# ScalarE for the first norm's second token block, and row halves that alternate in the indexer scores, in a two-layer fp32 decoder

## The chip, the cores and the metric

The kernel runs on one core of a Trainium2 chip. The metric is the device time of one execution, in microseconds (us). The time of the kernel before is 927.51 us, the median of 3 runs (927.25 to 927.71).

## What is computed

The reference is a post-norm decoder of two layers on 256 tokens of 1,024 channels, in fp32, with a LayerNorm ahead of the first layer. The parts that the change touches:

```python
h = _layer_norm(x, ln_in_g, ln_in_b)
# per layer: h <- LN(alpha*h + Mixer(h)); h <- LN(alpha*h + ConvGatedMLP(h))
# A: logits += cumsum(log sigmoid forget gate), causal softmax, times v
# B, the indexer that picks 64 keys per query:
r = relu(einsum('bqhd,bkd->bqhk', q_idx, k_idx) * DI ** -0.5)
score = einsum('bqhk,bqh->bqk', r, w_idx)
# C, differential attention:
p = softmax(s, axis=-1)
a = p[:, :, 0] - lam * p[:, :, 1]
o_c = _rms_norm(einsum('bhqk,bkhd->bqhd', a, v), diff_norm_g) * (1.0 - lam_init)
```

## The kernel before

**Weights.** About 80 MB of fp32 weights per layer stream through SBUF once. SyncE loads chunks of 512 KB into seven raw buffers. `Stream.split` (line 146) cuts each 128x512 piece into a high part, which ScalarE writes (hl <- raw), and a low part, which VectorE writes (raw minus high, hl <- raw, hl). Sixteen such pairs fit. TensorE then makes three fp32r matmuls per product (`mm3`): high x high, low x high, high x low. A pair is used by six matmuls of 512 columns, or by twelve of 256. The activations are split in the same way into hTh and hTl.

**Order.** The order of every engine's instructions is fixed when the program is built. The main line emits the weight matmuls, and after every few of them `Tasks.tick` (line 286) lets each live task, a Python generator, emit a piece of its work (attention, norms, rotary steps) and then calls `Stream.refill` (line 177), which may emit one split. When a task may go on is decided by the planner `Clocks` (line 197), which adds up modelled costs per engine. `ready(engine, tiles)` (line 387) holds a task until its inputs are done by these clocks, and also while VectorE's clock is more than 2.5 us ahead of TensorE's, and, for VectorE's tasks in the attention stage, while fewer than three pairs are split ahead. `refill` splits when fewer than `W.low` pairs are ahead, or when `W.hold` is off and VectorE's clock is not too far on. `W.low` is -1 during the first norm and LOW = 3 afterwards.

**Start.** `first_norm` (line 590) runs once per block of 128 tokens (tb = 0, 1): statistics, rs from GpSimd, two normalisations of 128x512, eight transposes on TensorE, two multiplications and additions with gb in PSUM on VectorE, then hTh (ScalarE) and hTl (VectorE). `spins` (line 585) are bf16 matmuls on a constant that nobody reads; tb = 0 has nine. The bank `warm` holds their output. Between the two calls the main line (lines 1316 to 1325) splits four pieces, two with the low part on VectorE and two on GpSimd. The rotary tables, on GpSimd and ScalarE, come behind.

**Attention.** `task_g1` (line 722) makes augL and augR, on 16 partitions, with which one matmul adds the forget-gate sums to A's logits (`task_A`, line 992: a mask matmul, the aug matmul, then the scores, for three banks per layer). `task_index` (line 859) makes the indexer's scores, 64 rows deep: heads with even numbers lie in the lower row half of the array, odd ones in the upper. A bank takes heads of one half; `par` runs two banks side by side. Relu (ScalarE) and a chain of multiply-adds into s (VectorE) follow, and then eight rounds of max and match-replace. `task_C` (line 1006) makes both softmaxes of differential attention, with the heads of the two halves in turn. `soften` (line 900) takes exponentials with their sums; the first softmax (a) is normalised there by eight operations, the second (p) is folded in by eight multiply-adds. `Square` with a sum and `crr` on GpSimd make the RMS norm of the product with v.

Every operation is issued from one helper line, L267.

Of the kernel before, what the change touches and what calls it, by code (L numbers as in the profile page):

```python
# [10 lines left out]
F32 = mybir.dt.float32  # L11
# [7 lines left out]
P = 128  # L19
# [92 lines left out]
class Stream:  # L112
# [32 lines left out]

    def split(self, lo=None):
        i = self.next_split
        if i >= len(self.items):
            return
        c, q, w = self.items[i]  # L150
        t = self.hl_pool.tile([P, 2, 512], R32, name=f"hl{i}", tag="hl")
        r = self.raw[c][:, q:q + w]
        clk = self.clocks.clk
        clk["ACT"] = max(clk["ACT"], self.free_at.get(i - HL_BUFS, 0))
        self.sc.activation(t[:, 0, :w], r, AF.Copy)
        (lo or self.ve).tensor_tensor(t[:, 1, :w], r, t[:, 0, :w].bitcast(F32), ALU.subtract)
        self.hl[i] = t
        self.next_split += 1
        if i + 1 == len(self.items) or self.items[i + 1][0] != c:
            del self.raw[c]  # L160
            self.split_at[c] = clk["DVE"]
            self.dma()

    def take(self):
# [31 lines left out]
class Clocks:  # L196
# [3 lines left out]
    def __init__(self):  # L200
        self.clk = dict(PE=0.0, DVE=0.0, ACT=0.0, POOL=0.0)
        self.done, self.by, self.read = {}, {}, {}
        self.table = "exp"

# [25 lines left out]
    def note(self, eng, op, args, kw):  # L230
# [8 lines left out]
        if op == "dma_start":  # L239
            self.done[out.name] = max(self.clk[eng], self.clk["PE"]) + 4000  # L240
            return
        start = max([self.clk[eng]] + [self.done.get(n, 0) for n in map(part, aps[1:]) if self.by.get(n) != eng])
        self.clk[eng] = start + self.cost(eng, op, out, aps)
        if "accum_out" in kw:
            self.clk[eng] += 155
# [70 lines left out]
def tile_hybrid(ctx: ExitStack, tc: tile.TileContext, a: dict, out: bass.AP):  # L316
# [273 lines left out]
    def first_norm(tb, st, hT, flag):  # L590

        mu, rs = ln_stats(st)
        if tb:
            yield
        for q in range(2):
            ve.tensor_scalar(h[tb][q], h[tb][q], mu, rs, ALU.subtract, ALU.mult)
        yield
        bks = []
        for q in range(2):
            yield from ready("PE", h[tb][q])  # L600
            bk = yield from att()
            bks.append(bk)
            transpose4(bk, h[tb][q])
            v = bk.rearrange("p (k t) -> p k t", k=4)
            for i, f in enumerate((ALU.mult, ALU.add)):
                ve.tensor_tensor(v, v, gb[:, i, 4 * q:4 * q + 4].unsqueeze(2).broadcast_to([P, 4, P]), f)
        if not tb:
            spins(9)
            att_free(warm)
        for q, bk in enumerate(bks):  # L610
            split_out(hT[0][:, 4 * q:4 * q + 4, tb * P:(tb + 1) * P],
                      hT[1][:, 4 * q:4 * q + 4, tb * P:(tb + 1) * P],
                      bk.rearrange("p (k t) -> p k t", k=4))
            att_free(bk)
            if not tb and not q:
                W.split(gp)
        flag.add(tb)
        W.hold = len(flag) < 2

    residual = set()  # L620
# [88 lines left out]
    def layer(l, hT, hflag):  # L709
# [12 lines left out]
        def task_g1(g1):  # L722
# [71 lines left out]
            t_ = t1([16, 256], "ct")  # L794
            augL = t1([16, 256], "augL", R32)
            augR = t4([16, 4, 256], R32, "augR")
            col = lambda i: cst[0:16, C_COL + i:C_COL + i + 1]
# [8 lines left out]
            for q in range(4):  # L806
                ve.tensor_scalar(augR[:, q, :], ch, cst[0:16, C_BM + q:C_BM + q + 1], None, ALU.mult)
            F["aug"] = (augL, augR)

# [49 lines left out]
        def task_index():  # L859
# [3 lines left out]
            s1 = t2([P, 256], n="s1")  # L863
            sx = [s0, s1]

            jobs = [(0, [0, 2, 4, 6]), (0, [1, 3, 5, 7]), (1, [0, 2]), (1, [1, 3]), (1, [4, 6]), (1, [5, 7])]

            def job(qb, hs):
                kw = P * (qb + 1)
                bk = yield from att()  # L870
                for n, i in enumerate(hs):
                    o = 64 * (i % 2)
                    mm(bk[:, n * kw:(n + 1) * kw], qiT[o:o + 64, i // 2, qb * P:(qb + 1) * P],
                       kiT[o:o + 64, 0:kw], n == 0)
                yield from ready("ACT", bk)
                rl = t2([P, len(hs), kw])
                sc.activation(rl, bk.rearrange("p (n k) -> p n k", n=len(hs)), AF.Relu)
                att_free(bk)
                for n, i in enumerate(hs):
                    prev = (m38[:, 256 - kw:256] if i == 0 else sx[qb])  # L880
                    ve.scalar_tensor_tensor(sx[qb], rl[:, n, :], biw[:, qb, i:i + 1], prev, ALU.mult, ALU.add)

            for i in range(0, 6, 2):
                yield from par(job(*jobs[i]), job(*jobs[i + 1]))
            mx = small([P, 2, 8], "mx")
# [13 lines left out]

        def soften(bk, ms, pt, rinv, norm=True):  # L900

# [3 lines left out]
            ve.tensor_reduce(mx[:, :len(ms)], v, AX.X, ALU.max, negate=True)  # L905
            sm = small([P, 4], "ssm")
            for n, m in enumerate(ms):
# [98 lines left out]
        def task_C():  # L1006
# [3 lines left out]
            a1, p1 = t4([P, 4, 256], n="a1"), t4([P, 4, 256], n="p1")  # L1010
            rina = small([P, 2, 4], "rina")
            rinv = small([P, 2, 4], "rinv")

            def scores(qb, ms):
# [5 lines left out]
                for n, m in enumerate(ms):  # L1020
                    for c in range(2):
                        mm(bks[c][:, n * kw:(n + 1) * kw],
                           qcT[64 * c:64 * c + 64, m, qb * P:(qb + 1) * P],
                           kcT[64 * c:64 * c + 64, m, 0:kw], False)
                yield from par(soften(bks[0], ms, (a0, a1)[qb], rina[:, qb, :]),
                               soften(bks[1], ms, (p0, p1)[qb], rinv[:, qb, :], norm=False))
            yield from par(scores(0, [0, 1, 2, 3]), scores(1, [0, 1]), scores(1, [2, 3]))
            ve.tensor_scalar(rinv, rinv, nlam[:, l:l + 1], None, ALU.mult)
            for qb, (pp, aa) in enumerate(((p0, a0), (p1, a1))):
                for m in range(4):  # L1030
                    ve.scalar_tensor_tensor(aa[:, m, :], pp[:, m, :], rinv[:, qb, m:m + 1], aa[:, m, :],
                                            ALU.mult, ALU.add)
            yield from ready("PE", a0, a1)
            q0 = t4([P, 4, 256], n="q0")
# [7 lines left out]
            def job(qb):  # L1042
# [356 lines left out]
```

## Time and profile before

| | before |
|---|---|
| median of 3 runs | 927.51 us (927.25 to 927.71) |
| profiled execution | 927.42 us |
| its span | 925.6 us |
| mean granted TensorE clock | 0.996 |
| TensorE matmul busy | 903.9 us |
| VectorE busy | 658.6 us |
| ScalarE busy | 510.4 us |
| GpSimd busy | 46.4 us |

A row of the timeline names the start, the duration of the group, the engine, the operation with its output and inputs, the shape and the count, and in brackets how long the engine sat idle before it and which engine released it. PE is TensorE's matmuls, PEld its weight loads, DVE is VectorE, ACT is ScalarE, POOL is GpSimd. An fp32 matmul stands as two records. Matmuls are pipelined, so the distance from start to start says what one costs; the duration is longer.

### The profile page before, as it was taken

How to read it: one execution, taken by the hardware profiler on the slowest of the kernel's cores; microseconds unless marked ns; L12 is line 12 of the kernel's file. 1: busy time of each engine (PE TensorE's matmuls, PEld its weight loads, DVE VectorE, ACT ScalarE, POOL GpSimd, SP SyncE). 2: the span in 40 equal slices, each digit the busy share in tenths (PEclk: the TensorE clock that was granted, in tenths of full speed). 3: DMA queues.
4: the chain of work that ended last, by engine and by line, in shares of the span. 5: the costliest groups of instructions: out<-in, count | busy, mean ns of one | idle time of the engine just before them, and what ended most of it. 6: DMA issues, size and time to landing. Idle time of an engine off the chain costs nothing. (4 is left out here: it accounts for less than half of the span.)

```text
span 925.6 us, 14457 instructions
## 1 busy us (share of the span) xinstructions
PE 903.9 (98%) x5329; PEld 787.8 (85%) x5329; DVE 658.6 (71%) x1283; ACT 510.4 (55%) x1006; POOL 46.4 (5%) x63
## 2 busy tenths in 40 slices
PE   7999999999999999999999999999999999999996
PEld 4877887888888999999988788888888799999995
DVE  7788677766678766766787956667667886766755
ACT  4754765655537655655455455665555375655540
POOL 6100000011000000000000000000110100000000
PEclk9999999999999999999999999999999999999999
DMA  8823356556636665565444323548675385566501
GB/s 289 303 91 114 95 171 231 193 199 221 204 122 225 215 200 187 180 200 182 131 157 152 113 91 114 188 138 286 187 245 172 119 277 186 177 192 186 180 18 46
DMA packets 46681, 161.47 MB, mean 174 GB/s; under 512 B 5841, under 2 KB 6865, under 8 KB 46609
## 3 DMA queue, kind: packets, MB, share of 16 engines
q1 hardware_dynamic: 44208, 155.20, 51.1%
q0 software_dynamic: 1408, 4.98, 1.7%
q8 instruction: 42, 0.69, 0.3%
q10 hardware_dynamic: 992, 0.35, 0.1%
q14 instruction: 31, 0.25, 0.1%
HBM read 159.47 MB, written 1.05 MB: 173 GB/s over the span
## 5 line engine op out<-in xcount | busy, mean ns | idle before, releaser
L267 DVE TENSOR_TENSOR hl<-raw,hl 128x512 fp32r<-128x512 f32 (+1 forms) x578 | 387.3, 696 | 186.6 <-ACT hl L267 184.7
L267 ACT ACTIVATE hl<-raw 128x512 fp32r<-128x512 f32 (+1 forms) x584 | 347.4, 625 | 192.9 <-PE att L267 94.1
L267 PE MATMUL acc<-hl,hTh 128*128 128x512 f32 (+1 forms) x896 | 276.8, 390 | 2.5 <-ACT hTh L267 2.1
L267 PE MATMUL att<-hTh,hl 128*128 128x256 f32 x1280 | 231.5, 283 | 0.0
L267 PEld LDWEIGHTS att<-hTh,hl 128*128 128x128 f32 x1280 | 200.8, 192 | 1.4
L267 PEld LDWEIGHTS acc<-hl,hTh 128*128 128x128 f32 x896 | 166.9, 188 | 37.7 <-ACT hTh L267 3.7
L267 PE MATMUL att<-hTl,hl 128*128 128x256 f32 x640 | 181.1, 283 | 0.0
L267 PE MATMUL acc<-hl,hTl 128*128 128x512 f32 (+1 forms) x448 | 165.5, 387 | 0.9 <-DVE hTl L267 0.9
L267 PE MATMUL acc<-hl,act 128*128 128x512 f32 x528 | 123.4, 390 | 0.0
L267 PEld LDWEIGHTS att<-hTl,hl 128*128 128x128 f32 x640 | 122.8, 192 | 0.0
L267 PEld LDWEIGHTS acc<-hl,act 128*128 128x128 f32 x528 | 97.9, 188 | 19.5
L267 PEld LDWEIGHTS acc<-hl,hTl 128*128 128x128 f32 x448 | 84.5, 189 | 17.7 <-DVE hTl L267 2.4
L267 PE MATMUL acc<-hl,oT 128*128 128x512 f32 x288 | 68.3, 391 | 0.0
L267 PEld LDWEIGHTS acc<-hl,oT 128*128 128x128 f32 x288 | 53.7, 188 | 10.9
L267 DVE SCALAR_TENSOR_TENSOR cv<-att,convp,cv 128x255 f32<-128x255 f32 x88 | 40.4, 480 | 16.1 <-ACT cv L267 14.5
L267 PE MATMUL acc<-hTh,hl 128*128 128x256 f32 x256 | 48.7, 289 | 3.0 <-DVE hl L267 2.6
L267 PE MATMUL acc<-hl,mT 128*128 128x512 f32 x192 | 45.4, 392 | 0.0
L267 PEld LDWEIGHTS acc<-hTh,hl 128*128 128x128 f32 x256 | 39.9, 191 | 5.5 <-DVE hl L267 3.2
L267 PEld LDWEIGHTS acc<-hl,mT 128*128 128x128 f32 x192 | 35.6, 188 | 7.1
L267 ACT ACTIVATE hTh<-att 128x512 fp32r<-128x512 f32 x16 | 9.6, 597 | 49.1 <-PE att L267 43.1
L267 PE MATMUL acc<-hTl,hl 128*128 128x256 f32 x128 | 36.2, 283 | 0.0
L267 ACT ACTIVATE t<-att 128x512 f32<-128x512 f32 (+1 forms) x32 | 18.2, 599 | 28.3 <-PE att L267 23.1
(162 smaller groups left out, 686.6 us busy)
## 6 DMA issues: line engine op xcount, KB each, us to landing
raw<-in_w_dram SPq DMA_DIRECT2D x284, 512.0 KB, 4.3
raw<-in_w_dram SPq DMA_DIRECT2D x8, 332.0 KB, 3.8
lng<-in_ln_g_dram POOLq DMA_DIRECT2D x4, 512.0 KB, 4.2
lnb<-in_ln_b_dram POOLq DMA_DIRECT2D x4, 512.0 KB, 5.5
h<-in_x_dram SPq DMA_DIRECT2D x4, 256.0 KB, 4.7
lng<-in_ln_in_g_dram SPq DMA_DIRECT2D x1, 512.0 KB, 8.1
lnb<-in_ln_in_b_dram SPq DMA_DIRECT2D x1, 512.0 KB, 10.2
wu<-in_w_ukv_dram POOLq DMA_DIRECT2D x2, 256.0 KB, 5.8
```

The costliest lines, as they stand in the source:

```text
L267: f(*args, **kw)
```

## The change

- In `first_norm`, for tb = 1, VectorE makes nmr = -mu x rs, and ScalarE normalises with Identity, scale rs and bias nmr. Five spins follow the transposes, and the bank warm is freed then. `W.low` becomes LOW only at the end of this call.
- The four splits around it have their low parts on VectorE; the last two of these come after nmr.
- The planner adds 110 ns to a VectorE operation that reads what the VectorE operation before it wrote.
- augL and augR get 128 partitions, zeroed by GpSimd, of which 16 are then written as before.
- An indexer job takes two banks, one per row half, and emits the heads of the halves in turn.
- Differential attention leaves both softmaxes unnormalised. The factor of p becomes -lambda x rinv x suma, and the norm of a enters by the scale of Square and by one multiplication of rr with rina. The eight multiply-adds are cut into pairs with a `ready` before and a yield after each.

```diff
-    def split(self, lo=None):
+    def split(self, lo=None, wait=False):
...
+        def low():
+            (lo or self.ve).tensor_tensor(t[:, 1, :w], r, t[:, 0, :w].bitcast(F32), ALU.subtract)
+        if not wait:
+            low()
...
+        if eng == "DVE" and self.prev in map(part, aps[1:]):
+            start += 110
...
         if tb:
             yield
+            nmr = small([P, 1], "nmr")
+            ve.scalar_tensor_tensor(nmr, mu, -1.0, rs, ALU.mult, ALU.mult)
         for q in range(2):
-            ve.tensor_scalar(h[tb][q], h[tb][q], mu, rs, ALU.subtract, ALU.mult)
+            if tb:
+                sc.activation(h[tb][q], h[tb][q], AF.Identity, bias=nmr, scale=rs)
+            else:
+                ve.tensor_scalar(h[tb][q], h[tb][q], mu, rs, ALU.subtract, ALU.mult)
...
-        if not tb:
-            spins(9)
+        spins((9, 5)[tb])
+        if tb:
             att_free(warm)
...
+        if tb:
+            W.low = LOW
...
-            augL = t1([16, 256], "augL", R32)
-            augR = t4([16, 4, 256], R32, "augR")
+            augL_ = t1([P, 256], "augL", R32)
+            augR_ = t4([P, 4, 256], R32, "augR")
+            gp.memset(augL_.bitcast(F32), 0.0)
+            gp.memset(augR_.bitcast(F32), 0.0)
+            augL, augR = augL_[0:16], augR_[0:16]
...
-            F["aug"] = (augL, augR)
+            F["aug"] = (augL_, augR_)
...
-                bk = yield from att()
+                bks = yield from att2()
                 for n, i in enumerate(hs):
-                    o = 64 * (i % 2)
-                    mm(bk[:, n * kw:(n + 1) * kw], qiT[o:o + 64, i // 2, qb * P:(qb + 1) * P],
-                       kiT[o:o + 64, 0:kw], n == 0)
...
+                    for c in range(2):
+                        o = 64 * c
+                        mm(bks[c][:, n * kw:(n + 1) * kw], qiT[o:o + 64, i // 2, qb * P:(qb + 1) * P],
+                           kiT[o:o + 64, 0:kw], n == 0)
...
-            for i in range(0, 6, 2):
-                yield from par(job(*jobs[i]), job(*jobs[i + 1]))
+            for qb, hs in ((0, [0, 2, 4, 6]), (1, [0, 2]), (1, [4, 6])):
+                yield from job(qb, hs)
...
-                yield from par(soften(bks[0], ms, (a0, a1)[qb], rina[:, qb, :]),
-                               soften(bks[1], ms, (p0, p1)[qb], rinv[:, qb, :], norm=False))
+                yield from par(soften(bks[0], ms, (a0, a1)[qb], rina[:, qb, :], False, suma[:, qb, :]),
+                               soften(bks[1], ms, (p0, p1)[qb], rinv[:, qb, :], False))
...
-            ve.tensor_scalar(rinv, rinv, nlam[:, l:l + 1], None, ALU.mult)
+            ve.scalar_tensor_tensor(rinv, rinv, nlam[:, l:l + 1], suma, ALU.mult, ALU.mult)
             for qb, (pp, aa) in enumerate(((p0, a0), (p1, a1))):
                 for m in range(4):
+                    if m % 2 == 0:
+                        yield from ready("DVE", pp)
                     ve.scalar_tensor_tensor(aa[:, m, :], pp[:, m, :], rinv[:, qb, m:m + 1], aa[:, m, :],
                                             ALU.mult, ALU.add)
+                    if m % 2:
+                        yield
...
                     sc.activation(oc[:, qb, m * P:(m + 1) * P], bk[:, m * P:(m + 1) * P], AF.Square,
-                                  accum_out=ssq[:, qb, m:m + 1])
+                                  scale=rina[:, qb, m:m + 1], accum_out=ssq[:, qb, m:m + 1])
...
+                ve.tensor_tensor(rr[:, qb, :], rr[:, qb, :], rina[:, qb, :], ALU.mult)
...
-    for e in (ve, ve, gp, gp):
+    for e in (ve, ve):
         W.split(e)
+    late_los = [W.split(ve, True) for _ in range(2)]
     T.tick()
-    W.low = LOW
+    for lo in late_los:
+        lo()
```

## Rows read from the trace of the kernel before

**Rows 1.** The page, part 1: busy us, share of the span, instructions.

```profile
PE 903.9 (98%) x5329; PEld 787.8 (85%) x5329; DVE 658.6 (71%) x1283; ACT 510.4 (55%) x1006; POOL 46.4 (5%) x63
```

**Rows 2.** PE's waits: who it waited for, us in total, times, longest.

```profile
PE att L267 <- DVE t L267: 3.4, 2, 1.8
PE acc L267 <- DVE hl L267: 2.6, 3, 1.4
PE att L267 <- DVE h L267: 2.1, 3, 1.1
```

**Rows 3.** Timeline of the start, both token blocks' norms (start us, us, engine, ...).

```profile
6.19 1.00 DVE L267 TENSOR_SCALAR h<-h,mv,rs 128x512 f32<-128x512 f32 x2 [0.67 <-POOL rs L267]
...
10.31 0.62 ACT L267 ACTIVATE hl<-raw 128x512 fp32r<-128x512 f32 x1
...
13.84 0.96 POOL L267 TENSOR_TENSOR rs<-mv,mhalf 128x1 f32<-128x1 f32 x1 [0.17 <-DVE mv L267]
...
14.77 2.77 POOL L267 TENSOR_TENSOR hl<-raw,hl 128x512 fp32r<-128x512 f32 x2
14.90 2.92 DVE L267 TENSOR_SCALAR h<-h,mv,rs 128x512 f32<-128x512 f32 x2
...
17.75 0.90 DVE L267 TENSOR_TENSOR hl<-raw,hl 128x332 fp32r<-128x332 f32 x2
...
18.58 2.75 DVE L267 TENSOR_TENSOR att<-att,gb 128x512 f32<-128x512 f32 x4
...
20.74 1.78 PE L267 MATMUL acc<-hl,hTh 128*128 128x512 f32 x4 [1.44 <-ACT hTh L267]
...
21.24 1.51 DVE L267 TENSOR_TENSOR hTl<-att,hTh 128x512 fp32r<-128x512 f32 x2
```

**Rows 4.** Windows of the start: PE, PEld, DVE, ACT, POOL busy, PEclk, DMA, GB/s.

```profile
18.00:21.10 3.10, 1.66 (x9) 1.14 (x10) 3.03 (x6) 0.60 (x1) 2.59 (x8) 1.00 0.77 258
21.10:24.50 3.40, 3.40 (x10) 2.58 (x9) 3.21 (x7) 3.06 (x6) 2.49 (x8) 0.50 0.93 210
```

**Rows 5.** Timeline of the index stage, first layer.

```profile
65.10 2.11 DVE L267 SCALAR_TENSOR_TENSOR s<-t,biw,s 128x256 f32<-128x256 f32 x4
...
72.11 1.07 PE L267 MATMUL att<-ident,t 128*128 128x128 f32 x8 [1.80 <-DVE t L267]
```

**Rows 6.** Timeline of differential attention, first layer.

```profile
112.92 0.87 DVE L267 TENSOR_SCALAR a<-a,rina 128x128 f32<-128x128 f32 x4
...
117.55 2.72 DVE L267 SCALAR_TENSOR_TENSOR a<-p,rinv,a 128x128 f32<-128x128 f32 x8
...
120.93 0.39 PE L267 MATMUL acc<-hTh,hl 128*128 128x256 f32 x1 [1.40 <-DVE hl L267]
```

**Rows 7.** Timeline of PE: scores of task_B (83.92 on), then of task_A (146.66 on).

```profile
83.92 0.39 PE L267 MATMUL att<-sb,negid 128*128 128x512 bf16 x1
84.15 1.05 PE L267 MATMUL att<-kbT,t 128*128 128x128 f32 x8
85.04 0.38 PE L267 MATMUL att<-sb,negid 128*128 128x512 bf16 x1
...
146.66 0.39 PE L267 MATMUL att<-m,negid 128*128 128x512 bf16 x1
...
148.41 0.27 PE L267 MATMUL att<-m,negid 128*128 128x256 bf16 x1
```

**Rows 8.** Timeline of PE: indexer scores (kiT,t), then differential scores (t,t), 64 rows.

```profile
56.94 1.71 PE L267 MATMUL att<-kiT,t 64*128 64x128 f32 x16
...
59.48 1.14 PE L267 MATMUL att<-kiT,t 64*128 64x256 f32 x8
...
97.56 1.16 PE L267 MATMUL att<-t,t 64*128 64x128 f32 x16
...
105.19 1.14 PE L267 MATMUL att<-t,t 64*128 64x256 f32 x8
```

**Rows 9.** Windows of the top-k stage, instructions on hl alone (columns as in Rows 4).

```profile
70.00:82.00 12.00, 9.37 (x42) 7.55 (x41) 3.41 (x5) 2.98 (x6) 0.00 (x0) 1.00 0.40 133
```

More of the change, by code (lines that the diff above doesn't have):

```diff
@@ L155, in split @@
         self.sc.activation(t[:, 0, :w], r, AF.Copy)
-        (lo or self.ve).tensor_tensor(t[:, 1, :w], r, t[:, 0, :w].bitcast(F32), ALU.subtract)
+        def low():
+            (lo or self.ve).tensor_tensor(t[:, 1, :w], r, t[:, 0, :w].bitcast(F32), ALU.subtract)
+        if not wait:
+            low()
         self.hl[i] = t
@@ L162, in split @@
             self.dma()
+        return low
     def take(self):
@@ L202, in __init__ @@
         self.done, self.by, self.read = {}, {}, {}
-        self.table = "exp"
+        self.table, self.prev = "exp", ""
     def cost(self, eng, op, out, args):
@@ L242, in note @@
         start = max([self.clk[eng]] + [self.done.get(n, 0) for n in map(part, aps[1:]) if self.by.get(n) != eng])
+        if eng == "DVE" and self.prev in map(part, aps[1:]):
+            start += 110
         self.clk[eng] = start + self.cost(eng, op, out, aps)
+        if eng == "DVE":
+            self.prev = part(out)
         if "accum_out" in kw:
@@ L864, in task_index @@
             sx = [s0, s1]
-            jobs = [(0, [0, 2, 4, 6]), (0, [1, 3, 5, 7]), (1, [0, 2]), (1, [1, 3]), (1, [4, 6]), (1, [5, 7])]
             def job(qb, hs):
                 kw = P * (qb + 1)
-                bk = yield from att()
+                bks = yield from att2()
                 for n, i in enumerate(hs):
-                    o = 64 * (i % 2)
-                    mm(bk[:, n * kw:(n + 1) * kw], qiT[o:o + 64, i // 2, qb * P:(qb + 1) * P],
-                       kiT[o:o + 64, 0:kw], n == 0)
[L875 to L881, printed above, removed]
-            for i in range(0, 6, 2):
-                yield from par(job(*jobs[i]), job(*jobs[i + 1]))
+                    for c in range(2):
+                        o = 64 * c
+                        mm(bks[c][:, n * kw:(n + 1) * kw], qiT[o:o + 64, i // 2, qb * P:(qb + 1) * P],
+                           kiT[o:o + 64, 0:kw], n == 0)
+                for c, bk in enumerate(bks):
+                    yield from ready("ACT", bk)
+                    rl = t2([P, len(hs), kw])
+                    sc.activation(rl, bk.rearrange("p (n k) -> p n k", n=len(hs)), AF.Relu)
+                    att_free(bk)
+                    for n, i in enumerate(hs):
+                        prev = (m38[:, 256 - kw:256] if i + c == 0 else sx[qb])
+                        ve.scalar_tensor_tensor(sx[qb], rl[:, n, :], biw[:, qb, i + c:i + c + 1], prev,
+                                                ALU.mult, ALU.add)
+                    yield
+            for qb, hs in ((0, [0, 2, 4, 6]), (1, [0, 2]), (1, [4, 6])):
+                yield from job(qb, hs)
             mx = small([P, 2, 8], "mx")
@@ L897, in task_index, with soften @@
             F["sel"] = (sb0, sb1)
-        def soften(bk, ms, pt, rinv, norm=True):
+        def soften(bk, ms, pt, rinv, norm=True, sums=None):
             yield from ready("DVE", bk)
@@ L905, in soften @@
             ve.tensor_reduce(mx[:, :len(ms)], v, AX.X, ALU.max, negate=True)
-            sm = small([P, 4], "ssm")
+            sm = small([P, 4], "ssm") if sums is None else sums[:, ms[0]:]
             for n, m in enumerate(ms):
@@ L1011, in task_C @@
             rina = small([P, 2, 4], "rina")
+            suma = small([P, 2, 4], "suma")
             rinv = small([P, 2, 4], "rinv")
@@ L1024, in scores @@
                            kcT[64 * c:64 * c + 64, m, 0:kw], False)
-                yield from par(soften(bks[0], ms, (a0, a1)[qb], rina[:, qb, :]),
-                               soften(bks[1], ms, (p0, p1)[qb], rinv[:, qb, :], norm=False))
+                yield from par(soften(bks[0], ms, (a0, a1)[qb], rina[:, qb, :], False, suma[:, qb, :]),
+                               soften(bks[1], ms, (p0, p1)[qb], rinv[:, qb, :], False))
             yield from par(scores(0, [0, 1, 2, 3]), scores(1, [0, 1]), scores(1, [2, 3]))
-            ve.tensor_scalar(rinv, rinv, nlam[:, l:l + 1], None, ALU.mult)
+            ve.scalar_tensor_tensor(rinv, rinv, nlam[:, l:l + 1], suma, ALU.mult, ALU.mult)
             for qb, (pp, aa) in enumerate(((p0, a0), (p1, a1))):
                 for m in range(4):
+                    if m % 2 == 0:
+                        yield from ready("DVE", pp)
                     ve.scalar_tensor_tensor(aa[:, m, :], pp[:, m, :], rinv[:, qb, m:m + 1], aa[:, m, :],
                                             ALU.mult, ALU.add)
+                    if m % 2:
+                        yield
             yield from ready("PE", a0, a1)
```

## Prediction

> **What bounds the kernel now.** I read the busy line of the page first. TensorE (PE) is busy for 98% of the span and no other engine for more than 71% [rows 1], so time is won only where PE idles or is made to run badly. Then I read what PE waited for: 3.4 us for a rotated tile t, 2.6 us for low halves of weights (hl) and 2.1 us for hTh of the first norm [rows 2]. Then I opened the timeline round each such wait, and the windows for the granted clock. Four places carry the sum.
>
> In the **first norm's second token block**, rs leaves POOL at 14.80. Two DVE normalisations then take 2.92 us, beside two POOL splits of 2.77 us that start 0.13 us earlier. The same pair for the first block, with POOL idle, took 1.00 us. Two splits of the next weights come next on DVE, the gb operations start at 18.58, and PE, idle for 1.44 us, gets hTh at 20.74 [rows 3]. PE was busy for only 1.66 of the 3.10 us up to 21.10, and for the next 3.40 us its granted clock is 0.50, the lower level (1.2 GHz) [rows 4].
>
> In the **index stage** PE stands 1.80 us for t. Its transposes were placed by the planner at a time when DVE was still working off a chain of dependent operations: four scores of 256 columns took 2.11 us, 0.53 each [rows 5], where the planner counts 110 + 1.2 x 256 = 417 ns. The other layer has the second of these waits, 3.4 us together [rows 2].
>
> In **differential attention** eight DVE operations in a row take 2.72 us, the low halves of weights queue behind them, and PE stands 1.40 us [rows 6]. There are two more waits for hl, 2.6 us over the three [rows 2]. The two **attention score forms** with few rows are in the part below.
>
> **The change, part by part.** The sum is made against the profiled execution (927.42 us, span 925.6), which lies 0.09 us under the median of the three runs.
>
> *First norm: -3.0 us.* The new chain is rs at 14.80, about 0.3 us for nmr on DVE and two hand-overs (the one from rs to h is 0.10 [rows 3]), then ScalarE. ScalarE took 0.62 us for 128x512 out of SBUF [rows 3], so the halves of h are ready near 15.7 and 16.3, where before they were ready at 14.90 + 1.46 = 16.4 and at 17.8. On DVE the two delayed low halves (0.65 each, as 2.75 / 4 is 0.69 for a like operation [rows 3]) end by 16.5, and the 0.90 us of splits ahead of gb are gone, because W.low now stays at -1 until the norm is through. So gb starts near 16.9 instead of 18.58: 1.7 us. PE's five added spins take about 0.22 us each, as 512 bf16 columns do from 83.92 to 84.15 [rows 7]. These 1.1 us fit between the transposes and the new hTh (near 18.8), so they cost nothing; without that cover they would cost 1.1. They also raise PE's activity ahead of the point where its clock fell. The 3.40 us at half clock lose 1.7 us, of which some 0.3 fall into a wait for hTl that stays (hTl's first half ends at 21.24 + 0.75 [rows 3]). With the clock kept that is 1.4 more, 3.1 in all, and I take 3.0. Bounds: -1.2 if the clock still falls and the transposes stand behind matmuls on PE's queue, -3.8 if all of it comes.
>
> The Trainium skill (VectorE: DVE Perf Modes, Specifications) places VectorE closer to SBUF and ScalarE closer to PSUM, which speaks against moving an SBUF-to-SBUF step to ScalarE. By that rule the move alone loses 0.2 to 0.5 us, and the undisturbed 1.00 us for two on DVE against 2 x 0.62 on ScalarE agrees [rows 3].
>
> *Indexer: -1.1 us.* Before, four heads on one row half are followed by four on the other: 16 matmul records take 1.71 us. The differential scores, which already alternate, take 1.16 us for 16 of the same shape [rows 8]: -0.55 us per layer. For the batches of eight both orders take 1.14 us [rows 8], so nothing moves there. Bounds 0 and -1.3.
>
> *Padding augL and augR to 128 rows: -2.3 us.* In task_A the mask of the first bank is at 146.66 and that of the next at 148.41: 1.75 us. task_B does the same without aug in 83.92 to 85.04: 1.12 us [rows 7]. The aug matmul thus costs 0.63 us, where 512 columns without a change of rows go on after 0.23 us. The other 0.40 us is paid for going from 128 rows to 16 and back; six such places give 2.4 us, and I take 2.3. All lie on PE, which has no idle time there. Bounds -1.2 (only the wait around the load goes) and -2.4. The two memsets per layer are new on POOL, and no row shows one. By the nearest rows, POOL splits of 1.39 us per 512 columns [rows 3], 1,280 columns cost 0 to 3.5 us. DVE's write of augL waits for them, and splits queue behind it on DVE. POOL idles there and starts while DVE does four small operations, so I take 0, with up to +2 in the range.
>
> The Trainium skill (GPSIMD Engine Reference, Key points) says that GpSimd shares its SBUF interface with VectorE and contends with it. By this the memsets slow DVE's work beside them by up to their own length. The trace shows the contention, 2.92 us against 1.00 [rows 3].
>
> *Planner's 110 ns and the pairs with yields: -2.5 and -2.6 us.* With 110 added, a score of 256 columns counts 527 ns, which is what it takes [rows 5]; the transposes are then placed after t is really there. Of 3.4 us I take 2.5, because DVE stays the scarce engine in that stage: in 12 us PE ran 42 matmuls on weights, seven pairs at six each, while DVE finished five [rows 9]. In differential attention the block of eight is cut into pairs, between which splits can go, and the normalisations of a (0.87 us for four [rows 6]) are dropped. That removes the 2.6 us of waits for hl. What is late next is again the low half of weights, at the pace of DVE. The extra rr x rina on four columns, the suma tile and the per-partition scale of Square lie off PE's path: 0, or +0.2 per layer if that cover goes. These two terms are bounded by +2 (the waits return elsewhere) and -6.5.
>
> Sum: -3.0 - 1.1 - 2.3 - 2.5 - 2.6 = -11.5; 927.42 - 11.5 = 915.9, with the 0.09 to the median 916.0 us.
>
> **The rivals.** (1) *DVE is the bound from the index stage on.* PE's saved waits come back as waits for low halves, because PE uses seven pairs while DVE makes five [rows 9]. Against it stands that DVE's own tasks are held back while fewer than three pairs are in stock (ready, line 387). Only the first norm, aug and the indexer stay: 927.5 - 6.4 = 921.1. (2) *The start gives little.* The clock falls in spite of the spins, or the splits held back until the norm ends are missing when g1 begins: 1.8 us less, 917.8. (3) *Slower.* The 110 ns make the planner believe DVE to be late everywhere, splits are emitted later, and PE enters the top-k rounds without stock. It then lacks two pairs in such 12 us, at 12 / 5 = 2.4 us each: 4.8 us per layer, 9.6 in all. With only the start, aug and the indexer won, that gives 927.5 - 6.4 + 9.6 = 930.7. It decides where fewer than two pairs are in stock at the start of the rounds. (4) *The edit doesn't do what it says:* 128 rows cost as much as 16, or the halves don't overlap: 916.0 + 3.4 = 919.4.
>
> **How the numbers follow.** Forecast 0.58, rival 1 0.22, rival 2 0.10, rival 3 0.05, rival 4 0.05. The range goes from 912.5 (916.0, less 0.8 at the start, 1.4 at the two wait terms, 0.3 at aug and the indexer, and 1.0 of the 2.1 us of waits for h [rows 2]) to 921.5, which takes in rivals 1, 2 and 4. A measurement of this kernel can tell about 0.2% (1.9 us) from no change. Faster by more than that, under 925.6, is nearly everything but rival 3 and a bad mixture of 1 with late memsets: 0.89. Within it 0.06, slower 0.05.
>
> **What would show it.** After: no half-clock stretch past 18 us and hTh on PE near 18.8; no gap of 0.4 us around the aug matmuls; 16 index records in about 1.15 us; no wait of PE for t near 70 and 520 us; no block of eight on DVE before the transposes of a. The prediction is wrong if PE's waits for hl grow beyond 5 us in all, or if PE's busy share falls in the stages of the top-k rounds.

## The result, and the profile after

| | before | after |
|---|---|---|
| median | 927.61 us of 4 runs (927.25 to 927.90) | 912.90 us of 4 runs (912.81 to 913.03) |
| ratio | | 0.9841 (0.9827 to 0.9855) |
| profiled execution | 927.42 us | 913.03 us |
| its span | 925.6 us | 911.2 us |

The change saves 14.7 us. The forecast was 916.0, and the time lies near the lower end of its range.

Both kernels run the same 4,656 matmuls on weights in the same order. So the start of the n-th of them in one trace can be subtracted from its start in the other. This shows where time goes, stage by stage:

| stage (times of before) | after less before, us |
|---|---|
| up to the first weight matmul (10.46) | -0.4 |
| from there to the 139th (47 us): first norm, first rotary steps | -2.4 |
| attention of layer 0 (to 167 us) | -6.0 |
| from there to the end of layer 1's attention (620 us) | -5.8 |
| the rest | +0.1 |

In the fourth line 0.5 us is lost at the norms between the two attentions and 6.3 are won in layer 1's attention itself. The first line is no gain: among the profiles of this study the first weight matmul starts anywhere from 9.8 to 11.0 us, even among kernels that are alike up to there (after 10.1, e3 10.8). Below, a kernel's trace is therefore measured from its first weight matmul to its last, which gives -14.0 us for after.

The busy line of the page of after (busy us, share of the span, instructions):

```profile
PE 898.0 (99%) x5334; PEld 786.7 (86%) x5334; DVE 652.1 (72%) x1272; ACT 512.1 (56%) x1008; POOL 46.4 (5%) x65
```

What PE waited for in after (us in total, times, longest):

```profile
PE acc L276 <- ACT hTh L276: 2.3, 7, 0.7
PE att L276 <- DVE h L276: 1.3, 1, 1.3
PE att L276 <- DVE spin L276: 1.1, 1, 1.1
```

PE is busy for 5.9 us less than in [rows 1], in a span that is 14.4 us shorter. The waits for t and for hl of [rows 2] are gone altogether, the one for h is down from 2.1 to 1.3, and the one for the first spins (1.0 in before) stays. All of PE's waits come to 4.7 us; before they came to 13.0 in eight groups, of which three stand in [rows 2]. The prediction gives 2.1 us for hTh there, but that row is for h. The row for hTh happens to have the same sum:

```profile
PE acc L267 <- ACT hTh L267: 2.1, 2, 1.4
```

Of the 2.3 us for hTh, 0.7 belong to the start. The other six waits, about 0.3 us each, are new and lie at the later norms.

The start of after, second block of tokens, from the timeline (answers to [rows 3]):

```profile
14.86 0.15 DVE L276 SCALAR_TENSOR_TENSOR nmr<-mv,rs 128x1 f32<-128x1 f32 x1
...
15.04 1.52 ACT L276 ACTIVATE h<-h,nmr,rs 128x512 f32<-128x512 f32 x2 [1.53 <-DVE nmr L276]
...
17.25 2.76 DVE L276 TENSOR_TENSOR att<-att,gb 128x512 f32<-128x512 f32 x4 [1.04 <-PE att L276]
...
19.42 1.19 PE L276 MATMUL acc<-hl,hTh 128*128 128x512 f32 x4 [0.70 <-ACT hTh L276]
```

ScalarE starts on h at 15.04, as counted, but takes 1.52 us for the two halves where the prediction counted 2 x 0.62. So gb starts at 17.25, 1.33 us earlier than before (forecast 1.7), and hTh reaches PE at 19.42 (forecast 18.8).

The windows of the start (answers to [rows 4]) and of the top-k stage (to [rows 9]); columns as there:

```profile
18.00:21.00 3.00, 2.27 (x10) 1.09 (x9) 2.83 (x5) 1.48 (x3) 2.40 (x10) 1.00 0.86 256
21.00:24.50 3.50, 3.50 (x17) 2.88 (x16) 0.65 (x2) 3.46 (x6) 2.04 (x8) 1.00 0.97 226
...
70.00:82.00 12.00, 12.00 (x55) 9.94 (x54) 5.81 (x9) 4.26 (x8) 0.00 (x0) 1.00 0.61 191
```

The clock stays at its upper level of 2.4 GHz. In the top-k stage PE now idles nowhere: 55 matmuls against 42, and VectorE makes nine low halves against five. VectorE itself has no more time for that, as the windows of all instructions show (before, then after; VectorE is the third figure behind the comma):

```profile
70.00:82.00 12.00, 10.20 (x50) 8.38 (x49) 11.96 (x51) 5.04 (x10) 0.00 (x0) 1.00 0.40 133
```

```profile
70.00:82.00 12.00, 12.00 (x55) 9.94 (x54) 12.00 (x44) 5.36 (x10) 0.00 (x0) 1.00 0.61 191
```

It works on other things, as its timeline shows. First two rows of before (the rotary step of t, set between two rounds of top-k), then after:

```profile
70.68 0.42 DVE L267 TENSOR_TENSOR ru<-t,cc 128x256 f32<-128x256 f32 x1
...
71.54 0.42 DVE L267 TENSOR_TENSOR t<-ru,rv 128x256 f32<-128x256 f32 x1
```

```profile
70.79 1.28 DVE L276 TENSOR_TENSOR hl<-raw,hl 128x512 fp32r<-128x512 f32 x2
71.99 0.61 DVE L276 MAX8 mx<-s 128x8 f32<-128x128 f32 x2
...
86.20 0.42 DVE L276 TENSOR_TENSOR ru<-t,cc 128x256 f32<-128x256 f32 x1
```

The rotary step has left the rounds; it comes at 86.20, when they are over, and the transposes of t, which waited at 72.11 [rows 5], come at 90 us and later. Most rounds now have two low halves behind them, and the last round ends at 84.5 instead of 81.9 us. The four more low halves, at 0.60 us from start to start, take the time of the rotary step (1.2 us) and of one round (1.2 us) that no longer fall into these 12 us. So the gain is not that t is ready in time at the old place: another place was chosen, and the rounds, for which PE shows no wait, run later.

Differential attention on VectorE (answers to [rows 6]):

```profile
116.96 0.60 DVE L276 SCALAR_TENSOR_TENSOR a<-p,rinv,a 128x128 f32<-128x128 f32 x2
117.49 0.68 DVE L276 TENSOR_TENSOR hl<-raw,hl 128x512 fp32r<-128x512 f32 x1
...
```

The pairs with low halves between them do what the diff says, and PE runs through. The indexer scores and the aug bank on PE (answers to [rows 8] and [rows 7]):

```profile
57.05 1.16 PE L276 MATMUL att<-kiT,t 64*128 64x128 f32 x16
...
59.72 1.14 PE L276 MATMUL att<-kiT,t 64*128 64x256 f32 x8
...
138.41 0.39 PE L276 MATMUL att<-m,negid 128*128 128x512 bf16 x1
138.45 0.58 PE L276 MATMUL att<-augR,augL 128*128 128x512 f32 x1
...
139.75 0.27 PE L276 MATMUL att<-m,negid 128*128 128x256 bf16 x1
```

Sixteen index records take 1.16 us instead of 1.71, and eights are unchanged. From mask to mask it is 1.34 us instead of 1.75. The new memsets, from GpSimd's timeline, and VectorE's first write of augL:

```profile
37.15 0.33 POOL L276 MEMSET augL<- 128x256 f32 x1
37.40 0.97 POOL L276 MEMSET augR<- 128x1024 f32 x1
...
46.82 0.47 DVE L276 SCALAR_TENSOR_TENSOR augL<-cl,cst,ct 16x256 fp32r<-16x256 f32 x1
```

They end 8 us before anyone needs them, and VectorE's two operations of eight columns beside them take 0.16 and 0.17 us, no more than a like one at 39.78 (0.16): cost 0, as taken.

### The profile page after: what moved, and what is told of

Its sections match the earlier page's. It is cut to its first block, busy times and chain, and to the rows that moved or that the text cites. A ratio compares the mean times of both kernels' runs of the same rounds, so it can differ in the third digit from the quotient of the medians.

```text
span 911.2 us, 14459 instructions
## 1 busy us (share of the span) xinstructions
PE 898.0 (99%) x5334; PEld 786.7 (86%) x5334; DVE 652.1 (72%) x1272; ACT 512.1 (56%) x1008; POOL 46.4 (5%) x65
## 5 line engine op out<-in xcount | busy, mean ns | idle before, releaser
L276 PEld LDWEIGHTS acc<-hl,oT 128*128 128x128 f32 x288 | 53.6, 188 | 10.8
L276 POOL TENSOR_TENSOR rs<-mv,mhalf 128x1 f32<-128x1 f32 x10 | 9.5, 948 | 485.0 <-DVE mv L276 485.0
L276 ACT ACTIVATE t<-acc 128x512 f32<-128x512 f32 (+1 forms) x36 | 20.1, 586 | 21.6 <-PE acc L276 20.8
```

Of the source, the lines that this page charges most:

```text
L276: f(*args, **kw)
```

## The experiments

Each is the changed kernel with one edit (e5 with two), except e2 and b_again, which start from before. "First to last" is the change between the first and the last weight matmul of the trace against before; "start" is the part of it up to the 139th; by then all these kernels have run the same other matmuls of the layer, the spins apart. Ratios are to runs of before on the same chip, whose medians lie between 927.4 and 927.7. Differences in time below are between the medians of this table, so some tenths of a microsecond in them can belong to the chip or to the time ahead of the first weight matmul.

| kernel | median us | ratio | start | first to last |
|---|---|---|---|---|
| after | 912.90 | 0.9841 (0.9827 to 0.9855) | -2.4 | -14.0 |
| e1_no110 | 914.99 | 0.9862 (0.9846 to 0.9878) | -2.0 | -12.6 |
| e2_only110 | 922.02 | 0.9941 (0.9926 to 0.9955) | -0.5 | -5.7 |
| e5_no110_old_jobs | 919.99 | 0.9918 (0.9903 to 0.9933) | -2.4 | -7.6 |
| e3_aug16 | 915.69 | 0.9872 (0.9857 to 0.9887) | -2.6 | -11.9 |
| e4_halves_in_blocks | 914.09 | 0.9855 (0.9840 to 0.9870) | -2.7 | -13.1 |
| c1_block_of_eight | 914.98 | 0.9863 (0.9849 to 0.9878) | -2.7 | -12.9 |
| c2_normalised | 913.54 | 0.9846 (0.9830 to 0.9863) | -2.5 | -14.0 |
| s1_no_spins | 912.92 | 0.9843 (0.9829 to 0.9858) | -2.7 | -14.4 |
| s2_dve_normalises | 914.82 | 0.9862 (0.9847 to 0.9876) | -2.1 | -12.5 |
| s3_pool_lows | 914.94 | 0.9864 (0.9849 to 0.9878) | -1.6 | -12.2 |
| s4_low_early | 915.09 | 0.9865 (0.9849 to 0.9882) | -1.6 | -12.1 |
| b_again | 927.22, one run | | 0.0 | 0.0 |

Five kernels with the same start as after (after, e3, e4, c1, c2) give -2.4 to -2.7 there, so 0.3 us is what two starts can differ by for nothing.

### The planner's count: e1, e2, e5

e1 takes the count out of after:

```diff
-            start += 110
+            start += 0
```

> The changed kernel without the 110 ns that its planner adds for a VectorE operation which reads the one before it. Theory (the truer count removes the two stands of TensorE for the rotated tile, because the transposes are placed later): the two waits come back, 3.4 to 3.7 us in all, and the time is 916 to 917 us (912.9 + 3.7). Rival (the stands went with the new job order of the indexer, which yields between the two halves, and the planner's count does nothing): no wait of TensorE for t, 912.5 to 913.5 us.

Measured: +2.1 us in time, but PE's waits for t do not come back; only 0.6 us stands for t, at the first rotary step. From first to last it is 1.5. The time lies between the two ranges expected, and on the waits the rival came true: in after, the count is not what removes them.

e2 puts the count alone into the kernel before:

```diff
...
+        if eng == "DVE" and self.prev in map(part, aps[1:]):
+            start += 110
...
+        if eng == "DVE":
+            self.prev = part(out)
```

> The kernel before with the planner's 110 ns alone. Theory: the two waits for t go and the waits for low halves in differential attention shrink in part, since its block of eight dependent operations is counted 0.9 us longer: 927.6 - 3.7 = 924 us, down to 922 if the latter go too. Rival (VectorE is the scarce engine; what is saved there comes back as waits for low halves): 926.5 to 927.6 us, with waits for hl of 5 us or more.

Measured: -5.4 us in time against before on the same chip (927.40), more than twice what e1 gave back. What PE waited for in e2:

```profile
PE acc L271 <- DVE hl L271: 1.1, 2, 0.6
...
PE att L271 <- DVE t L271: 0.5, 1, 0.5
```

VectorE's rotary step and PE's transposes in the timeline of e2:

```profile
69.07 0.42 DVE L271 TENSOR_TENSOR ru<-t,cc 128x256 f32<-128x256 f32 x1
...
70.49 1.07 PE L271 MATMUL att<-ident,t 128*128 128x128 f32 x8
```

Here the count removes the waits, but not as the prediction had it, by later transposes. It moves the step that t needs: the rotary step starts at 69.07, one round of top-k earlier than the 70.68 of before, and the transposes, still at their old place, find t ready. Waits for t fall by 2.9 us, waits for hl by 1.5.

What removed the waits in e1, then? e5 is e1 with the indexer's jobs as they were (six jobs of one bank, two side by side):

```diff
-            start += 110
+            start += 0
...
-            for qb, hs in ((0, [0, 2, 4, 6]), (1, [0, 2]), (1, [4, 6])):
-                yield from job(qb, hs)
+            for i in range(0, 6, 2):
+                yield from par(job(*jobs[i]), job(*jobs[i + 1]))
```

> The changed kernel without the 110 ns and with the indexer's old jobs (one bank each, side by side, heads of one half in a block). Theory (the new jobs had taken over the count's part, since they yield more often and so spread the chain of scores): the two waits for t come back, 3.4 us or more, with the 1.1 us for the order of the halves 915.0 + 4.5 = 919.5 us. Rival (something else in the change keeps the waits away): no wait for t over 0.6 us, 915.5 to 916.5 us.

Measured: +5.0 us against e1, of which the halves' order explains 1.1 (e4 below). PE's waits for t are 4.0 us in three, and one is back at its old place, as PE's timeline of e5 shows:

```profile
70.06 1.06 PE L276 MATMUL att<-ident,t 128*128 128x128 f32 x8 [1.83 <-DVE t L276]
```

So either the count or the new jobs remove the waits for t, and only with both missing do they return. With the new jobs the rotary step and its transposes land behind the rounds, in e1 (transposes from 86.72 on) as in after. That the jobs' new yields do it is argued, not shown: which part of the new jobs it is was not tried.

### The matmul forms: e3, e4

e3 gives augL and augR their 16 partitions back:

```diff
-            augL_ = t1([P, 256], "augL", R32)
-            augR_ = t4([P, 4, 256], R32, "augR")
-            gp.memset(augL_.bitcast(F32), 0.0)
-            gp.memset(augR_.bitcast(F32), 0.0)
-            augL, augR = augL_[0:16], augR_[0:16]
+            augL = t1([16, 256], "augL", R32)
+            augR = t4([16, 4, 256], R32, "augR")
...
-            F["aug"] = (augL_, augR_)
+            F["aug"] = (augL, augR)
```

> The changed kernel with augL and augR on 16 partitions again and without the two memsets per layer. Theory (0.40 us of TensorE for each of six changes from 128 rows to 16 and back): 912.9 + 2.4 = 915.3 us, the aug matmuls again at 0.43 us from start to start and their masks at 0.31 and 0.20. Rival (the memsets on GpSimd cost what the rows save): within 0.5 us of 912.9.

PE's timeline of e3:

```profile
138.93 0.39 PE L276 MATMUL att<-m,negid 128*128 128x512 bf16 x1
139.25 0.49 PE L276 MATMUL att<-augR,augL 16*128 16x512 f32 x1
...
140.66 0.27 PE L276 MATMUL att<-m,negid 128*128 128x256 bf16 x1
```

Measured: +2.8 us in time, 2.2 from first to last. From start to start the aug matmuls, the masks and the scores next to them cost 2.39 us more in both layers, 0.40 for each of the six places. The rows show where: aug starts 0.32 us after its mask where it starts 0.04 after it in after, and the distance from mask to mask is 1.73 us again. The Trainium skill (TensorEngine Tiling (Array Packing), Key Properties) says that a change of the tiling mode drains TensorE. It gives no price; the trace agrees, with 0.40 us for going from 128 rows to 16 and back, if that counts as a change of mode.

e4 keeps the new jobs and swaps the two loops, so that the heads of one half come first:

```diff
-                for n, i in enumerate(hs):
-                    for c in range(2):
+                for c in range(2):
+                    for n, i in enumerate(hs):
```

> The changed kernel, its indexer jobs with two banks as they are, but all matmuls of one row half ahead of all of the other. Theory (overlap comes from the order alone): 16 records take 1.64 us from start to start again instead of 1.09, the batches of eight stay at 1.07: 912.9 + 1.1 = 914.0 us. Rival (it is the two banks per job, not the order): 912.9 us, 1.09 us for 16 records.

PE's timeline of e4:

```profile
57.23 1.71 PE L276 MATMUL att<-kiT,t 64*128 64x128 f32 x16
...
60.45 1.14 PE L276 MATMUL att<-kiT,t 64*128 64x256 f32 x8
```

Measured: +1.2 us in time (1.0 from first to last) and +1.09 from start to start on the groups of 16, over both layers. Both the 1.71 us and the 1.14 us of [rows 8] are back to the last digit: the order of halves matters for 128 columns and not for 256.

### Differential attention: c1, c2

c1 takes the pairs away:

```diff
-                    if m % 2 == 0:
-                        yield from ready("DVE", pp)
...
-                    if m % 2:
-                        yield
```

> The changed kernel with the eight multiply-adds of differential attention in one block again (no ready, no yield between them), softmaxes unnormalised, the planner's 110 ns kept. Theory (the cut into pairs lets the low halves through): one wait of TensorE for hl of 0.7 to 1.5 us per layer comes back, 914.3 to 915.9 us. Rival (dropping the normalisations and the truer count are enough): no wait over 0.3 us there, 912.5 to 913.3 us.

The timelines of VectorE and PE in c1:

```profile
116.86 2.72 DVE L276 SCALAR_TENSOR_TENSOR a<-p,rinv,a 128x128 f32<-128x128 f32 x8
...
120.24 0.39 PE L276 MATMUL acc<-hTh,hl 128*128 128x256 f32 x1 [0.61 <-DVE hl L276]
```

Measured: +2.1 us in time, of which 0.6 stand ahead of the first weight matmul. The block of 2.72 us is back, and with it one wait for hl per layer, 1.1 us in both by the profile. Their gaps from start to start are 0.78 and 0.65 us longer than in after, 1.4 us together; from first to last it is 1.2. That is less than the waits for hl of before: e2, which has the block but also the count, has the same two waits of 1.1 us. So the block accounts for 1.1 to 1.4 us, and the rest of the 2.6 us of [rows 2] is what the count alone removed in e2.

c2 normalises a in `soften` again and keeps the pairs:

```diff
-                yield from par(soften(bks[0], ms, (a0, a1)[qb], rina[:, qb, :], False, suma[:, qb, :]),
+                yield from par(soften(bks[0], ms, (a0, a1)[qb], rina[:, qb, :]),
...
-                                  scale=rina[:, qb, m:m + 1], accum_out=ssq[:, qb, m:m + 1])
+                                  accum_out=ssq[:, qb, m:m + 1])
...
-                ve.tensor_tensor(rr[:, qb, :], rr[:, qb, :], rina[:, qb, :], ALU.mult)
```

> The changed kernel with the first softmax of differential attention normalised in soften again (eight VectorE operations per layer, about 2.1 us, in place of one of four columns), the multiply-adds still in pairs. Theory (the pairs and the count removed the waits, VectorE has room): 912.5 to 913.5 us. Rival (VectorE is so scarce there that its 2.1 us per layer come out at TensorE): waits for hl of 2 us or more per layer, 915 to 917 us.

Measured: -14.0 us from first to last, as after, and no wait for hl. The 0.6 us in the median stand ahead of the first weight matmul. The unnormalised softmax is worth nothing that can be measured here.

### The start: s1 to s4, and before once more

s1 leaves the five added spins out:

```diff
-        spins((9, 5)[tb])
-        if tb:
+        if not tb:
+            spins(9)
```

> The changed kernel without the five spins of the second block (the bank warm is freed after the first block again). Theory (the spins keep the granted clock up): a stretch at 0.50 comes back behind 19 us, some 3.4 us long, and costs 1.4 us: 914.3 us. Rival (the earlier transposes and matmuls are enough, the spins only fill a wait): the clock stays at 1.00 and the time is 912.5 to 913.0 us.

The windows of the start of s1:

```profile
18.00:21.00 3.00, 1.22 (x7) 0.71 (x5) 2.93 (x5) 0.87 (x2) 2.36 (x9) 1.00 0.93 335
21.00:24.50 3.50, 3.46 (x16) 2.66 (x15) 1.33 (x3) 3.45 (x6) 2.18 (x10) 1.00 0.80 198
```

Measured: the same time as after. PE is busy for 1.22 of 3.00 us, less than in before, and the granted clock stays at 1.00. So the spins cost nothing that can be measured, and here they do not hold the clock up either.

s2 lets VectorE normalise the second block:

```diff
-            nmr = small([P, 1], "nmr")
-            ve.scalar_tensor_tensor(nmr, mu, -1.0, rs, ALU.mult, ALU.mult)
...
-            if tb:
-                sc.activation(h[tb][q], h[tb][q], AF.Identity, bias=nmr, scale=rs)
-            else:
-                ve.tensor_scalar(h[tb][q], h[tb][q], mu, rs, ALU.subtract, ALU.mult)
+            ve.tensor_scalar(h[tb][q], h[tb][q], mu, rs, ALU.subtract, ALU.mult)
```

> The changed kernel with VectorE normalising the second block as before, but with no split on GpSimd beside it. Theory (the gain lies in GpSimd's splits being gone and in W.low, not in ScalarE): the pair takes 1.0 us instead of 2.92, the two late low halves come 0.9 us later and TensorE's last matmuls of the first block with them: 912.9 to 913.9 us. Rival (GpSimd's small operations for the rotary tables slow VectorE's pair as its splits did): 2.5 us or more for the pair, 914.5 to 915.5 us.

VectorE's and PE's timelines of s2:

```profile
14.50 1.00 DVE L276 TENSOR_SCALAR h<-h,mv,rs 128x512 f32<-128x512 f32 x2
...
18.79 1.20 PE L276 MATMUL acc<-hl,hTh 128*128 128x512 f32 x4 [0.74 <-ACT hTh L276]
...
23.65 4.01 DVE L276 TENSOR_TENSOR hl<-raw,hl 128x332 fp32r<-128x332 f32 x9 [2.85 <-ACT hl L276]
...
109.08 0.38 PE L276 MATMUL acc<-hTh,hl 128*128 128x256 f32 x1 [0.34 <-DVE hl L276]
```

Measured: with GpSimd's splits out of the way VectorE takes 1.00 us for the pair, not the 2.92 of [rows 3], and hTh is on PE sooner: 4.39 us behind the end of rs on GpSimd (14.40), against 4.66 in after (rs ends at 14.76). So the move to ScalarE by itself loses 0.3 us here, within the 0.2 to 0.5 that the prediction gave for the move alone. The time lies in the rival's range all the same, for other reasons. By the 139th weight matmul s2 is 0.3 to 0.6 us behind kernels with ScalarE's step, because nine low halves, not eight as in after, stand ahead of the first rotary step. Another 1.1 us is lost in layer 0, near 108 us among other places, where two waits for weights appear (0.28 and 0.34 us); 0.4 of the 1.9 us in time does not show in this profile. s3 and s4 have the same two waits and lose the same 1.1: a start that ends otherwise sends the planner another way through layer 0 (from the 165th weight matmul on TensorE's order is not that of after in all three). That part says nothing on the edit.

s3 has two of the four low halves on GpSimd again and none delayed:

```diff
-    for e in (ve, ve):
+    for e in (ve, ve, gp, gp):
         W.split(e)
-    late_los = [W.split(ve, True) for _ in range(2)]
     T.tick()
-    for lo in late_los:
-        lo()
```

> The changed kernel with the last two low halves on GpSimd again, ScalarE normalising. Theory: the two low halves end near 17.5 us instead of 16.2, TensorE's last matmuls of the first block wait for them, the transposes stand behind in the queue, and the second block starts about 1.0 to 1.3 us later: 914.0 us. Rival (the transposes go ahead and the chain through gb doesn't notice): 912.9 us.

GpSimd's and VectorE's timelines of s3:

```profile
14.55 2.60 POOL L276 TENSOR_TENSOR hl<-raw,hl 128x512 fp32r<-128x512 f32 x2
14.69 1.25 DVE L276 SCALAR_TENSOR_TENSOR nmr<-mv,rs 128x1 f32<-128x1 f32 x1
```

Measured: the start loses 0.7 to 1.1 us, but not in the way expected. One operation on a single column takes 1.25 us beside GpSimd's splits, 0.15 without them, and h waits for it. Yet gb starts at 17.54, only 0.3 us later than in after, with the first weight matmul at the same time. The rest is lost behind the norm, on ScalarE: three splits now stand ahead of its table load for the sines, which starts at 22.12 instead of 20.72 (see the last run), and the first rotary step's transposes come at 30.33 instead of 29.57.

s4 sets `W.low` to LOW where it was set before:

```diff
-        if tb:
-            W.low = LOW
...
     for lo in late_los:
         lo()
+    W.low = LOW
```

> The changed kernel with W.low at LOW right after the delayed low halves, as it was. Theory: splits of the next weights go ahead of gb on VectorE again, 0.45 us each, two to four of them, and hTh comes 0.9 to 1.8 us later: 913.8 to 914.7 us. Rival (they fill idle time of VectorE and give the next weights a lead): 912.5 to 912.9 us.

VectorE's and PE's timelines of s4:

```profile
16.93 1.35 DVE L276 TENSOR_TENSOR hl<-raw,hl 128x332 fp32r<-128x332 f32 x3 [0.76 <-ACT hl L276]
18.20 2.75 DVE L276 TENSOR_TENSOR att<-att,gb 128x512 f32<-128x512 f32 x4
...
20.37 1.20 PE L276 MATMUL acc<-hl,hTh 128*128 128x512 f32 x4 [1.66 <-ACT hTh L276]
```

Measured: three splits come ahead of gb, hTh reaches PE at 20.37 instead of 19.42, and the start loses 0.8 to 1.1 us.

The last run is the kernel before, unchanged, with a second profile.

> The kernel before, profiled again. Theory (its start has so little work on TensorE up to 21 us that the clock falls each time): again a stretch of 3.4 us at a granted clock of 0.50. Rival (whether it falls differs from one execution to the next): 1.00 throughout, and TensorE's last weight matmul 1.0 to 1.6 us earlier after the start.

Windows of the start in this second profile of before:

```profile
18.00:21.10 3.10, 1.66 (x10) 1.09 (x9) 3.03 (x7) 0.60 (x1) 2.51 (x9) 1.00 0.85 288
21.10:24.50 3.40, 3.37 (x15) 2.49 (x14) 2.99 (x6) 3.29 (x6) 2.34 (x7) 1.00 0.98 191
```

PE's transposes of the first rotary step in its timeline:

```profile
31.52 1.06 PE L267 MATMUL att<-ident,t 128*128 128x128 f32 x8 [1.36 <-DVE t L267]
```

Measured: PE is busy for the same 1.66 us ahead of 21.10 as in [rows 4], and this time the granted clock stays at 1.00. Yet nothing is won. PE now stands 1.36 us for t at the first rotary step, where the first profile has the same transposes at 31.75 with no such wait. The 139th weight matmul is at the same distance from the first in both profiles, to 0.05 us, and so is the last. The half clock of the first profile was paid out of a wait that came anyway: the chain up to the first rotary step set the end of the start. Part of this chain is ScalarE, as rows of before show:

```profile
21.91 1.58 ACT L267 ACTIVATE hl<-raw 128x332 fp32r<-128x332 f32 x4
23.51 1.28 ACT L267 ACT_TABLE_LOAD   x1
...
27.07 2.79 DVE L267 TENSOR_TENSOR hl<-raw,hl 128x332 fp32r<-128x332 f32 x5 [2.62 <-ACT hl L267]
```

and the same place in after:

```profile
20.72 1.28 ACT L276 ACT_TABLE_LOAD   x1
...
24.28 3.41 DVE L276 TENSOR_TENSOR hl<-raw,hl 128x332 fp32r<-128x332 f32 x8 [2.85 <-ACT hl L276]
```

Behind hTh ScalarE loads a table for the sines of the rotary tables, computes them, loads a table again (1.28 us each) and only then goes on with high halves, for which VectorE stands 2.6 to 2.9 us. In before four splits go ahead of the first load, in after none, so the load starts 2.8 us earlier where hTh is 1.3 us earlier. The Trainium skill (TensorE: Matmul & The Clock Gate, What's actually happening) says that the gate's observation is not tied to the start of the kernel, so that the point where the clock changes differs from run to run. The two profiles of one program go further: the clock fell in one and not in the other.

## Why the prediction was right, and where it was not

The bound, the four places and the direction were right, and no rival came about. VectorE did not become the bound (rival 1, 921.1), the start did not give little (rival 2), nothing became slower (rival 3), and the matmul forms did what they say (rival 4). The forecast sum was -11.5; measured between the profiled executions is -14.4. That the time lies in the range is in part luck: the two wait terms together won more than their own bound of -6.5 allowed, while the start gave less than forecast and the norms behind the attentions lost 0.7 us that it did not count.

**First norm, -3.0; measured -2.4 to -2.7.** The size was nearly right, half of the reason was wrong. The 1.7 us of earlier gb became 1.33, mostly because the two Identity operations took 1.52 us and not 2 x 0.62. The 1.4 us for a kept clock did not exist: in b_again the clock is kept in the unchanged kernel, and the time is the same. The failed step is that a half-clock stretch was priced by its length without asking what PE met next. What did shorten the chain was shown by s3 (no splits on GpSimd: 0.7 to 1.1) and s4 (no early splits ahead of gb: 0.8 to 1.1). ScalarE's step is not a gain by itself: in s2 VectorE's pair brings hTh 0.3 us sooner, and the 0.3 to 0.6 that s2 is behind later comes from one more low half ahead of the rotary step. The prediction also left out ScalarE's part behind hTh: with no split there, the table loads come earlier. No run changes that alone. The transposes of the first rotary step come at 29.57 instead of 31.5 to 31.75. The spins were rightly costed at nothing, but their part in the clock was not seen in s1.

**Indexer, -1.1.** Measured 1.09 on the records and 1.0 to 1.2 in time (e4). Right.

**Aug, -2.3.** Measured 2.39 on the records (e3), within its bound of -2.4; of the 2.8 in time, 0.7 stand ahead of e3's first weight matmul. Right. The memsets cost nothing, as taken.

**The two wait terms, -2.5 and -2.6.** These were mis-sized. The two attentions won 12.3 us (6.0 and 6.3); less 2.4 for aug and 1.1 for the indexer, 8.8 are left, where 5.1 were forecast and 6.5 were the bound. Two steps failed. First, the prediction kept 0.9 of the 3.4 us back because VectorE "stays the scarce engine in that stage". But five low halves in 12 us was no limit of the engine: VectorE was full in both kernels (11.96 and 12.00 us), and what changed is what it was given. With the rotary step and one round out of these 12 us it made nine. What the prediction itself put against rival 1, that VectorE's own tasks are held back while few pairs are in stock, fits with this; no run tests it. Second, the waits that the profile lists are not all that is lost. In before, from start to start, PE lost 3.7 us around the two waits listed with 3.4, and 3.8 us around the waits for hl in differential attention, where [rows 2] list 2.6. These 7.5 us are gone; some 1.3 of the 8.8 are spread over smaller gaps that no run separates.

**The planner's mechanism.** The prediction said that with 110 ns the transposes are placed after t is really there. In before alone (e2) the count works the other way round, with the rotary step one round earlier. In after the new indexer jobs are enough by themselves (e1). As each can do the work of the other, undoing one thing at a time does not add up: e5 gives back 6.4 us (first to last) with the count and the jobs, e3 2.2, c1 1.2, and the start is worth 2.4. Together that is 12.2 of 14.0. The missing 1.8 us have no single owner in these runs.

**Signs.** Of those listed, the clock, the aug gap, the index records, the waits for t and the block of eight came as said; hTh was 0.6 us later than said. New and not foreseen are the waits for hTh at the later norms, about 0.3 us each. They seem to come with the count: e2, with the count alone, lists eight waits for hTh, and e1, without it, only two, 1.3 us in all.

## What to carry to other kernels

Before pricing a slow stretch, look for the next wait behind it, and take a second profile of the same program: a half clock whose time comes out of a wait for VectorE costs nothing. Where a planner orders the work by modelled costs, compare them with start-to-start distances of dependent operations, and judge edits to its tasks by the order that comes out, since 1 us can move with an edit that has nothing to do with it. On the engine that feeds the weights, cut blocks of some 2.7 us into pairs, and see what else it does where it is busy all the time: work that nobody waits for can come later. On TensorE keep the number of rows the same from matmul to matmul (0.40 us per place here), and with 64 rows and 128 columns alternate the row halves (0.55 us per 16 records here).

## What the runs showed of the hardware

- The granted clock fell to 0.50 in one profile of before and stayed at 1.00 in another, after the same 1.66 us of PE activity in 3.10; in s1 it stayed at 1.00 after 1.22 in 3.00.
- Beside two-input splits on GpSimd a one-column VectorE operation took 1.25 us instead of 0.15 (s3). It has one column to read and write, so its own amount of data does not set this price. It ended at 15.94, as the first of the two splits did (14.55 + 1.37 = 15.92), which looks like a wait for the whole split; that was not tested.
- GpSimd's memset of 128x1024 fp32 takes 0.97 us and of 128x256 0.33, far under the 3.5 us that its splits gave as a bound.
- Two Identity operations of ScalarE on 128x512, with scale and bias per partition, take 1.52 us; three plain copies in a row, hl<-raw at 11.79 in after, take 1.72.
